# The opening of a hybrid decoder layer: token tiles ahead of weights, weight splits by halves, and one more load buffer

## The chip, the cores and the metric

One NeuronCore of a Trainium2 chip runs the whole program. The metric is the device time of one execution in microseconds (us), smaller is better. The kernel computes in float32 and takes each matrix product apart: every operand is split into an upper part (float32 rounded to the matrix engine's fp32r form) and a lower part (what is left), and a product is three passes: upper by upper, upper by lower, lower by upper.

Engines: PE is the matrix engine (its results go to PSUM banks), ACT the scalar engine, DVE the vector engine, POOL the general one, SP the queue that issues most loads.

## The reference

One layer on 512 tokens of 1024 channels:

```python
h = rms_norm(x, norm_mix_g)
p = h @ w_in                    # q_a, k_a, v_a, o_a, i_a, f_a, q_b, k_b, v_b, g_a, g_b
qk_a = silu(causal_conv(concat(q_a, k_a), conv_w))
h_a = mlstm_chunkwise(q_a, k_a, v_a, i_a + b_i, f_a + b_f)
y_a = sigmoid(o_a) * head_rms_norm(h_a)
y_b = stick_breaking(norm(q_b), norm(k_b), v_b)
y = sigmoid(g_a + b) * y_a + sigmoid(g_b + b) * y_b
x = x + y @ w_out
x = x + square(relu(rms_norm(x) @ w_up)) @ w_down
```

This case touches the first lines: the normalisation of x, its transposes, and the first column block of `v_a`, called va0; and the loads of the first q, k pairs of the second mixer, called qkb0.

## The kernel before, in words

Tokens lie in four tiles of 128 (t = 0 to 3). A tile's opening steps are: square and root on ACT with the reciprocal on DVE (`q`, L259 to L261); scaling by the root and by the gain on DVE in two halves of 512 channels (`s`, L267), each followed by four PE transposes into a bank `pt` (L271); the upper part of the turned half on ACT (`u`, L282) and the lower part on DVE (`l`, L286), both written into `hT`. Weights of va0 come in four pairs (256 rows of `w_in`, two k-slices of 128, 512 KB): the upper part is cast on ACT (`w`, L290), the lower part taken on DVE (`v`, L293). The gain is spread over the partitions by PE into two banks `gps` of the pool `ps_proj` (four banks), which the scaling reads until the last tile.

The order of these steps on ACT and DVE is written out as a string, which `opening` follows: each step is put behind the last one of its engine. Where PE's products stand is chosen by a planner from estimated times; `issue_after` and the argument `behind` add constraints. Engines then run their instructions in that order. `keep_warm(n)` issues n dummy products on a tile `warm` into the bank `pw`, of the pool `ps_a` (also four banks), after some of the transposes.

`chunk("va0", ...)` makes the products of va0 for one token tile o at a time as the planner sees it: eight k-slices of three passes (L120, L121, L122 of `mm3`), accumulated in a bank `pp`, then evacuated and split. Before the fourth tile come the products of the gates, `pg` (L316), which need the whole of `hT`.

SP issues the loads in program order of the planner: the gain `gx`, then for each i the token tile x i (L196) and the weight pair w i (`raw_va`, L198), then the columns of the gates (L367) and the pairs of the first mixer's q, k (`raw_qka`, L111).

Later, `stage` loads a pair into a buffer `raw`, and casts it (L115, L116). Up to qkb0 the buffers are two of the pool `wp`, in turn, so that the third pair is loaded after the first has been split. From qkb1 on a third buffer, in the pool `at`, takes part. The matrix products `za` of the first mixer (L452, L454), which read `qh`, `ql` and `kk`, start within the products of qkb1.

Of the kernel before, what the change touches and what calls it, by code (L numbers as in the profile page):

```python
# [8 lines left out]
F32 = mybir.dt.float32  # L9
F32R = mybir.dt.float32r  # L10
# [6 lines left out]
P = 128  # L17
S = 512
D = 1024
NT = S // P  # L20
NK = D // P
# [43 lines left out]
def block_kernel(ctx: ExitStack, tc: tile.TileContext, x, norm_mix_g, w_in, b_if, b_gate, conv_w, mlstm_norm_g,  # L65
                 sb_q_norm_g, sb_k_norm_g, w_out, norm_mlp_g, w_up, w_down, out):
    nc = tc.nc
    act, dve, pool, pe = nc.scalar, nc.vector, nc.gpsimd, nc.tensor
# [3 lines left out]
    wp = ctx.enter_context(tc.tile_pool(name="wp", bufs=4))  # L72
    r4 = ctx.enter_context(tc.tile_pool(name="r4", bufs=12))
    sm = ctx.enter_context(tc.tile_pool(name="sm", bufs=2))
    ps_proj = ctx.enter_context(tc.tile_pool(name="ps_proj", bufs=4, space=PSUM))
# [6 lines left out]
    def bank(name):  # L82
        return ps_a.tile([P, S], F32, tag="pa", name=name)
# [14 lines left out]
        return at.tile([P, S], F32, tag=tag, name=name, bufs=bufs)  # L98


    last, load_pool, staged = {}, [(wp, "raw", 2)], []

    def stage(k2, srcs, name, ahead=None, pool_raw=None):

        with tc.high_priority(offset=AHEAD if ahead is None else ahead):
            p, tag, bufs = load_pool[len(staged) % len(load_pool)] if pool_raw is None else (pool_raw, "raw", 2)
            staged.append(name)
            raw = p.tile([P, 2, 512], F32, tag=tag, name=f"raw_{name}{k2}", bufs=bufs)
            for c, ap in srcs:
                n = ap.shape[-1]  # L110
                last["load"] = nc.sync.dma_start(out=raw[:, :, c:c + n],  # L111
                                                 in_=ap.rearrange("(kk p) n -> p kk n", p=P)).ins
            hi = wp.tile([P, 2, 512], F32R, tag="whi", name=f"whi_{name}{k2}")
            lo = wp.tile([P, 2, 512], F32R, tag="wlo", name=f"wlo_{name}{k2}")
            act.copy(hi, raw)  # L115
            dve.tensor_sub(lo, raw, hi.bitcast(F32))  # L116
        return hi, lo

    def mm3(o, ah, al, bh, bl, start, stop, **kw):
        pe.matmul(o, ah, bh, start=start, stop=False, **kw)  # L120
        pe.matmul(o, ah, bl, start=False, stop=False, **kw)  # L121
        return pe.matmul(o, al, bh, start=False, stop=stop, **kw).ins  # L122

    def chunk(name, src, transposed, lhs=None, staged=None, evac=None, gen=False,
              order=range(4), behind={}):


        acc = {}

        def one(o, k, wh, wl):  # L130
            kk, sl = k % 2, slice(o * P, (o + 1) * P)
            st, sp = k == 0, k == NK - 1
            if transposed:
                mm3(acc[o], wh[:, kk, sl], wl[:, kk, sl], hT[0][:, k, :], hT[1][:, k, :], st, sp)
            else:
                ah, al = (hT[0][:, k, sl], hT[1][:, k, sl]) if lhs is None else lhs(k, sl)
                mm3(acc[o], ah, al, wh[:, kk, :], wl[:, kk, :], st, sp)

        def new(o):
            acc[o] = ps_proj.tile([P, S], F32, tag="pp", name=f"pp_{name}{o}")  # L140

        if evac is not None:
            w = staged or [stage(k2, src(k2), name) for k2 in range(4)]
            def each():
                for o in order:
                    new(o)
                    for k in range(NK):
                        with ExitStack() as es:
                            if k in behind:
                                es.enter_context(tc.issue_after(behind[k]))  # L150
                            one(o, k, *w[k // 2])
                    evac(o, acc[o])
                    yield
            if gen:
                return each()
            list(each())
        else:
            for o in range(4):
                new(o)
            for k2 in range(4):  # L160
                w = staged[k2] if staged else stage(k2, src(k2), name)
                for k in (2 * k2, 2 * k2 + 1):
                    for o in range(4):
                        one(o, k, *w)
        return list(acc.values())

    def in_cols(*parts):
        def src(k2):
            c, got = 0, []
            for c0, n in parts:  # L170
                got.append((c, w_in[0, k2 * 256:(k2 + 1) * 256, c0:c0 + n]))
                c += n
            return got
        return src
# [4 lines left out]
    def split(dst, val):  # L179

        act.copy(dst[:, 0, :], val)
        return dve.tensor_sub(dst[:, 1, :], val, dst[:, 0, :].bitcast(F32)).ins
# [3 lines left out]
    xp = first.enter_context(tc.tile_pool(name="xp", bufs=1, side="right"))  # L186
# [4 lines left out]
    gx = xp.tile([1, D], F32, name="gx")  # L191
    nc.sync.dma_start(out=gx, in_=norm_mix_g[0:1, :])
    xs, raw_va, va0_src = {}, {}, in_cols((C_VA, 512))
    for i in range(NT):
        xs[i] = xp.tile([P, D], F32, name=f"x_{i}")
        nc.sync.dma_start(out=xs[i], in_=x[0, i * P:(i + 1) * P, :])  # L196
        raw_va[i] = (xp if i < 2 else wp).tile([P, 2, 512], F32, tag="raw", name=f"raw_va0{i}", bufs=2)
        last["load"] = nc.sync.dma_start(out=raw_va[i], in_=va0_src(i)[0][1].rearrange("(kk p) n -> p kk n", p=P)).ins  # L198
    eps = cst.tile([P, 1], F32, name="eps")
    pool.memset(eps, EPS)  # L200
    one1 = xp.tile([P, P], F32R, name="one1")
# [25 lines left out]
    pw = bank("pw")  # L227

    def keep_warm(n):
        for i in range(n):  # L230
            pe.matmul(pw, warm[:, :P], warm, start=True, stop=True)
# [3 lines left out]
    for i in range(2):  # L235
        c = slice(i * S, (i + 1) * S)
# [9 lines left out]
    r_, xn_, pt_, va0_w, tail = {}, {}, {}, {}, {i.engine: i for i in (gain_hi, gain_lo)}  # L246

    def in_turn(f, *args):

        with ExitStack() as es:  # L250
            for i in tail.values():
                es.enter_context(tc.issue_after(i))
            for i in f(*args):
                tail[i.engine] = i
# [8 lines left out]
    def o_scale(t, g):  # L263
        if g == 0:
            xn_[t] = xp.tile([P, D], F32, tag="nx", name=f"xn{t}", bufs=3)
        c = slice(g * S, (g + 1) * S)
        yield dve.scalar_tensor_tensor(xn_[t][:, c], xs[t][:, c], r_[t], gps[g], ALU.mult, ALU.mult).ins  # L267
        pt_[t, g] = bank(f"pt{t}{g}")
        for i in range(4):
            k = 4 * g + i  # L270
            turned = pe.transpose(pt_[t, g][:, i * P:(i + 1) * P], xn_[t][:, k * P:(k + 1) * P], ident).ins  # L271
        last["turned", t, g] = turned
        with tc.issue_after(turned):
            keep_warm({(0, 0): 1, (0, 1): 5, (1, 0): 3}.get((t, g), 0))

    def h_part(t, g):
        return [h[:, 4 * g:4 * g + 4, t * P:(t + 1) * P] for h in hT], pt_[t, g][:, :].rearrange(
# [7 lines left out]
        (hi, lo), p3 = h_part(t, g)  # L285
        yield dve.tensor_sub(lo, p3, hi.bitcast(F32)).ins  # L286

    def o_weights(i):
        va0_w[i] = tuple(wp.tile([P, 2, 512], F32R, tag=f"w{w}", name=f"w{w}_va0{i}") for w in ("hi", "lo"))
        yield act.copy(va0_w[i][0], raw_va[i]).ins  # L290

    def o_weights_lower(i):
        yield dve.tensor_sub(va0_w[i][1], raw_va[i], va0_w[i][0].bitcast(F32)).ins  # L293

    def o_gates():
        for i in range(2):
# [4 lines left out]
    def opening(steps):  # L301
        kinds = {"q": o_square, "s": o_scale, "u": o_upper, "l": o_lower, "w": o_weights, "v": o_weights_lower,
                 "g": o_gates}
        with tc.high_priority(offset=URGENT):
            for n in steps.split():
                in_turn(kinds[n[0]], *(int(i) for i in n[1:]))
# [49 lines left out]
    v0, v1 = [], []  # L356

    def v_evac(got, name):
        def evac(o, acc):
            v = r4.tile([P, 2, S], F32R, tag="r4", name=f"{name}{o}")  # L360
            split(v, acc)
            got.append(v)
        return evac

    wr = cv.tile([P, NK, 16], F32, name="wg_r")
    with tc.issue_after(last["load"]):
        nc.sync.dma_start(out=wr, in_=w_in[0, :, C_I:C_I + 16].rearrange("(k p) n -> p k n", p=P))  # L367
    wg = r4.tile([P, 2, S], F32R, tag="r4", name="wg")[:, :, :].rearrange("p w (k n) -> p (w k) n", k=4)
    pool.memset(wg.bitcast(F32), 0.0)
    opening("q0 s00 s01 u00 l00 w0 v0 q1 s10 u01 l01 s11 u10 l10 w1 v1 u11 l11 q2 s20 s21 w2 v2 u20 l20 q3 s30 u21 "  # L370
            "s31 l21 w3 v3 u30 g l30 u31 l31")
    va0 = chunk("va0", None, False, staged=va0_w, evac=v_evac(v0, "va0"), gen=True,
                behind={k: last["turned", k // 2, 1] for k in range(4, NK)})
    next(va0)
    next(va0)
    next(va0)
# [267 lines left out]
    at = late.enter_context(tc.tile_pool(name="at", bufs=1, reuse_waits="tile"))  # L644
# [4 lines left out]
        pool.memset(oh[:, h, h:h + 1], 1.0)  # L649
    oh_r = at.tile([P, 8, 8], F32R, name="oh_r")  # L650
    pool.tensor_copy(oh_r, oh)
    msk = at.tile([P, S], F32, name="msk")
    pool.memset(msk, 0.0)
    pool.memset(msk[:, 384:], 1.0)
# [69 lines left out]
    def parts(n, t, own=False):  # L724
        hi, lo = (r4.tile([P, 2, S], F32R, tag="r4", name=f"w{w}_{n}") if own else
                  wp.tile([P, 2, S], F32R, tag=f"w{w}", name=f"w{w}_{n}") for w in ("hi", "lo"))
        act.copy(hi, t)
        dve.tensor_sub(lo, t, hi.bitcast(F32))  # L728
        return hi, lo
# [141 lines left out]
    with tc.high_priority(offset=AHEAD):  # L871
        w0 = [parts(f"p1up0{j}", buf0["X", j], True) for j in range(2)]
# [118 lines left out]
```

## Time and profile before

| | us |
|---|---|
| median of 3 runs (lowest, highest) | 816.85 (816.73, 817.37) |
| the profiled execution | 816.42 |
| its span, first to last instruction | 814.4 |
| PE busy | 805.7 |
| DVE busy | 599.8 |
| ACT busy | 457.1 |
| POOL busy | 164.6 |

A row of the timeline gives the start (us from the start of the span), the time of the group, engine, line, operation, the tile written and the tiles read, and how many instructions were merged; in brackets stand the idle time of the engine ahead of it and what ended it. A row of the windows gives the stretch, its length, busy time and count for PE, weight loads, DVE, ACT and POOL (an engine without work in the question asked is left out), the granted clock, the DMA share and GB/s. A row of the loads gives the target, the queue, the count, the size and the time from issue to landing. PE's matmuls are pipelined, and their ends are modelled: what one costs is the step from start to start.

### The profile page before, as it was taken

To read this page: it belongs to the slowest core of one execution; us is meant where nothing else is said; L and a number is where in the kernel's file an instruction comes from. 1 tells how busy PE (TensorE), PEld (TensorE's weight loads), DVE (VectorE), ACT (ScalarE), POOL (GpSimd) and SP (SyncE) were. 2 spreads that over 40 slices of the span, in tenths; PEclk is the share of its full clock that TensorE was granted. 3 is DMA by queue.
4 is the path that set the end of the run, shared out by engine and by line. 5 is a ranking of instruction groups with operands and counts; after the bars stand their busy time and mean duration, and the time that the engine had idled before them with its cause. 6 is when DMAs were issued, how large, how long until landed. Compare 5 with 4: busy or idle time off the path is not lost.

```text
span 814.4 us, 11569 instructions
## 1 busy us (share of the span) xinstructions
PE 805.7 (99%) x4392; PEld 693.5 (85%) x4392; DVE 599.8 (74%) x828; ACT 457.1 (56%) x681; POOL 164.6 (20%) x216
## 2 busy tenths in 40 slices
PE   8999999999999999999999999999999999999998
PEld 6878887888888887888888888999999899999876
DVE  6669967684598486756753659898689868978995
ACT  6429756654557467545542537576455635755642
POOL 3014323111221240010120101223302330232220
PEclk9999999999999999999999999999999999999999
DMA  9454542343433423522257506987977995999964
GB/s 225 98 155 147 123 77 63 88 98 85 150 93 93 120 62 70 137 72 77 78 182 263 124 1 158 208 177 159 204 228 161 179 208 182 182 198 184 233 120 119
DMA packets 64552, 113.65 MB, mean 140 GB/s; under 512 B 5809, under 2 KB 18401, under 8 KB 64498
## 3 DMA queue, kind: packets, MB, share of 16 engines
q1 hardware_dynamic: 44914, 71.43, 31.6%
q0 software_dynamic: 19584, 41.50, 26.8%
q8 instruction: 34, 0.56, 0.3%
q14 instruction: 20, 0.16, 0.1%
HBM read 110.74 MB, written 2.17 MB: 139 GB/s over the span
## 4 chain that ended last, share of the span: by engine, by line
PE 92%; DVE 5%; ACT 1%; issue 1%; DMA 0%; SPq 0%; DVEq 0%; ACTq 0%
PE pp_qkb L122 4%; PE pp_qkb L120 4%; PE pp_qkb L121 4%; PE pp_yup L120 3%; PE pp_yup L121 3%; PE pp_yup L122 3%; PE ydn L121 2%; PE ydn L122 2%; PE ydn L120 2%; PE pp_qka L120 2%; PE pp_va L121 2%; PE pp_qka L121 2%; PE pp_ga L121 2%; PE pp_vb L122 2%; PE pp_vb L120 2%; PE pp_oa L122 2%
## 5 line engine op out<-in xcount | busy, mean ns | idle before, releaser
L561 POOL TENSOR_SCALAR_AFFINE_SELECT b<-b 128x128 f32<-128x128 f32 x32 | 19.0, 608 | 161.2 <-ACT b L558 161.2
L121 PE MATMUL pp_qkb<-wlo_qkb,hT 128*128 128x512 f32 x128 | 50.2, 392 | 0.0
L122 PE MATMUL pp_qkb<-whi_qkb,hT 128*128 128x512 f32 x128 | 50.1, 394 | 0.0
L120 PE MATMUL pp_qkb<-whi_qkb,hT 128*128 128x512 f32 x128 | 49.4, 392 | 0.0
L767 POOL DMA_DIRECT2D raw_Xup<-in_w_up_dram x24 | 28.9, 1239 | 84.8 <-DVE wlo_p5up L728 37.2
L767 POOL DMA_DIRECT2D raw_Xdn<-in_w_down_dram x18 | 21.6, 1214 | 102.8 <-DVE wlo_p5dn L728 36.4
L566 DVE TENSOR_TENSOR_SCAN r<-r,msk 128x512 f32<-128x512 f32 (+3 forms) x32 | 25.1, 833 | 14.5 <-ACT r L558 14.5
L116 DVE TENSOR_TENSOR wlo_qkb<-raw_qkb,whi_qkb 128x1024 fp32r<-128x1024 f32 x16 | 21.7, 1364 | 13.8 <-ACT whi_qkb L115 13.8
L122 PEld LDWEIGHTS pp_qkb<-whi_qkb,hT 128*128 128x128 f32 x128 | 24.1, 188 | 5.1
L120 PEld LDWEIGHTS pp_qkb<-whi_qkb,hT 128*128 128x128 f32 x128 | 24.1, 188 | 5.1
L121 PEld LDWEIGHTS pp_qkb<-wlo_qkb,hT 128*128 128x128 f32 x128 | 24.1, 188 | 4.7
L913 ACT ACTIVATE uq<-uq 128x512 f32<-128x512 f32 x32 | 20.0, 630 | 12.2 <-DVE uq L912 12.0
L121 PE MATMUL pp_va<-wlo_va,hT 128*128 128x512 f32 x64 | 24.9, 392 | 0.8 <-DVE wlo_va L293 0.8
L120 PE MATMUL pp_ga<-hT,whi_ga 128*128 128x512 f32 x64 | 25.3, 395 | 0.0
L120 PE MATMUL pp_qka<-hT,whi_qka 128*128 128x512 f32 x64 | 25.2, 397 | 0.0
L121 PE MATMUL pp_qka<-hT,whi_qka 128*128 128x512 f32 x64 | 25.2, 394 | 0.0
L121 PE MATMUL pp_wo<-wlo_wo,y 128*128 128x512 f32 x64 | 25.1, 392 | 0.0
L121 PE MATMUL pp_ga<-hT,whi_ga 128*128 128x512 f32 x64 | 25.1, 392 | 0.0
L121 PE MATMUL pp_oa<-hT,whi_oa 128*128 128x512 f32 x64 | 25.1, 392 | 0.0
L122 PE MATMUL pp_oa<-hT,wlo_oa 128*128 128x512 f32 x64 | 25.1, 392 | 0.0
L120 PE MATMUL pp_vb<-whi_vb,hT 128*128 128x512 f32 x64 | 25.1, 392 | 0.0
L121 PE MATMUL pp_gb<-hT,whi_gb 128*128 128x512 f32 x64 | 25.1, 392 | 0.0
(578 smaller groups left out, 2962.1 us busy)
## 6 DMA issues: line engine op xcount, KB each, us to landing
raw_Xup<-in_w_up_dram POOLq DMA_DIRECT2D x24, 512.0 KB, 7.3
raw_Xdn<-in_w_down_dram POOLq DMA_DIRECT2D x18, 512.0 KB, 6.6
raw_qkb<-in_w_in_dram SPq DMA_DIRECT2D x32, 256.0 KB, 3.9
rb<-rows POOLq DMA_DIRECT2D x8, 640.0 KB, 5.5
raw_va<-in_w_in_dram SPq DMA_DIRECT2D x8, 512.0 KB, 5.2
raw_qka<-in_w_in_dram SPq DMA_DIRECT2D x16, 256.0 KB, 6.3
raw_vb<-in_w_in_dram SPq DMA_DIRECT2D x8, 512.0 KB, 4.4
raw_oa<-in_w_in_dram SPq DMA_DIRECT2D x8, 512.0 KB, 4.2
```

Source lines behind the costliest of these rows:

```text
L116: dve.tensor_sub(lo, raw, hi.bitcast(F32))
L120: pe.matmul(o, ah, bh, start=start, stop=False, **kw)
L121: pe.matmul(o, ah, bl, start=False, stop=False, **kw)
L122: return pe.matmul(o, al, bh, start=False, stop=stop, **kw).ins
L561: pool.affine_select(out=b[:, d], in_=b[:, d], pattern=[[-1, P]], compare_op=ALU.is_gt, fill=0.0, base=0, channel_multiplier=1)
L566: dve.tensor_tensor_scan(kr, kr, msk[:, S - n:][:, ::-1], 1.0, ALU.mult, ALU.max)
L767: pool.dma_start(out=buf[b, j], in_=src(more, j), accum_op=ALU.add)
L913: act.activation(h(r, c), h(r, c), AF.Square)
```

## The change

- The loads are issued as x0, x1, w0, w1, x2, w2, x3, w3 (before x0, w0, x1, w1, ...).
- In the string of steps, tile 1's square comes right after tile 0's on ACT, tile 1's scaling is mixed with tile 0's lower parts, and the pairs 0, 1 and 2 of the weights are cast and split by halves (one k-slice each: `w00`, `w01`, `v00`, `v01`).
- Within `mm3`, va0 makes the pass lower rows by upper weights ahead of upper rows by lower weights.
- The third tile's sums go to the bank `pw`, the dummies' one, instead of a new bank of `ps_proj`.
- The products of tile 1, k-slice 3, are put behind tile 2's first transposes on PE.
- After tile 0's second transposes stand three dummies instead of five.
- The third pair of qkb0 is loaded into the buffer of `at`.

```diff
+    last, load_pool, staged, at_once = {}, [(wp, "raw", 2)], [], {}
...
+            p, tag, bufs = at_once.get((name, k2), (p, tag, bufs))
...
-    def mm3(o, ah, al, bh, bl, start, stop, **kw):
+    def mm3(o, ah, al, bh, bl, start, stop, rows_first=False, **kw):
         pe.matmul(o, ah, bh, start=start, stop=False, **kw)
-        pe.matmul(o, ah, bl, start=False, stop=False, **kw)
-        return pe.matmul(o, al, bh, start=False, stop=stop, **kw).ins
+        two = ((ah, bl), (al, bh))
+        for i, (a, b) in enumerate(two[::-1] if rows_first else two):
+            end = pe.matmul(o, a, b, start=False, stop=stop and i == 1, **kw).ins
+        return end
...
-            acc[o] = ps_proj.tile([P, S], F32, tag="pp", name=f"pp_{name}{o}")
+            acc[o] = banks.get(o) or ps_proj.tile([P, S], F32, tag="pp", name=f"pp_{name}{o}")
...
-                            if k in behind:
-                                es.enter_context(tc.issue_after(behind[k]))
+                            for i in (k, (o, k)):
+                                if i in behind:
+                                    es.enter_context(tc.issue_after(behind[i]))
...
-    for i in range(NT):
-        xs[i] = xp.tile([P, D], F32, name=f"x_{i}")
...
+    for n in "x0 x1 w0 w1 x2 w2 x3 w3".split():
...
-            keep_warm({(0, 0): 1, (0, 1): 5, (1, 0): 3}.get((t, g), 0))
+            keep_warm({(0, 0): 1, (0, 1): 3, (1, 0): 3}.get((t, g), 0))
...
+    def o_weights(i, h=None):
+        if not h:
+            va0_w[i] = tuple(wp.tile([P, 2, 512], F32R, tag=f"w{w}", name=f"w{w}_va0{i}") for w in ("hi", "lo"))
+        c = slice(None) if h is None else slice(h, h + 1)
+        yield act.copy(va0_w[i][0][:, c], raw_va[i][:, c]).ins
...
-    opening("q0 s00 s01 u00 l00 w0 v0 q1 s10 u01 l01 s11 u10 l10 w1 v1 u11 l11 q2 s20 s21 w2 v2 u20 l20 q3 s30 u21 "
-            "s31 l21 w3 v3 u30 g l30 u31 l31")
-    va0 = chunk("va0", None, False, staged=va0_w, evac=v_evac(v0, "va0"), gen=True,
-                behind={k: last["turned", k // 2, 1] for k in range(4, NK)})
+    opening("q0 s00 s01 q1 u00 s10 l00 s11 w00 u10 v00 w01 l10 v01 u01 u11 l01 l11 w10 v10 w11 v11 q2 s20 s21 w20 u20 v20 "
+            "w21 l20 v21 q3 s30 s31 u21 l21 w3 v3 u30 g l30 u31 l31")
+    va0 = chunk("va0", None, False, staged=va0_w, evac=v_evac(v0, "va0"), gen=True, banks={2: pw}, behind={
+        **{k: last["turned", k // 2, 1] for k in range(4, NK)}, (1, 3): last["turned", 2, 0]})
...
+    at_once["qkb0", 2] = (at, "raw", 1)
```

More of the change, by code (lines that the diff above doesn't have):

```diff
@@ L98, in t2 @@
         return at.tile([P, S], F32, tag=tag, name=name, bufs=bufs)
-    last, load_pool, staged = {}, [(wp, "raw", 2)], []
+    last, load_pool, staged, at_once = {}, [(wp, "raw", 2)], [], {}
     def stage(k2, srcs, name, ahead=None, pool_raw=None):
@@ L117, in stage @@
         return hi, lo
-    def mm3(o, ah, al, bh, bl, start, stop, **kw):
+    def mm3(o, ah, al, bh, bl, start, stop, rows_first=False, **kw):
         pe.matmul(o, ah, bh, start=start, stop=False, **kw)
-        pe.matmul(o, ah, bl, start=False, stop=False, **kw)
-        return pe.matmul(o, al, bh, start=False, stop=stop, **kw).ins
+        two = ((ah, bl), (al, bh))
+        for i, (a, b) in enumerate(two[::-1] if rows_first else two):
+            end = pe.matmul(o, a, b, start=False, stop=stop and i == 1, **kw).ins
+        return end
     def chunk(name, src, transposed, lhs=None, staged=None, evac=None, gen=False,
-              order=range(4), behind={}):
+              order=range(4), behind={}, banks={}):
         acc = {}
@@ L136, in one @@
                 ah, al = (hT[0][:, k, sl], hT[1][:, k, sl]) if lhs is None else lhs(k, sl)
[L137 removed]
+                mm3(acc[o], ah, al, wh[:, kk, :], wl[:, kk, :], st, sp, name == "va0")
         def new(o):
[L140 removed]
+            acc[o] = banks.get(o) or ps_proj.tile([P, S], F32, tag="pp", name=f"pp_{name}{o}")
         if evac is not None:
@@ L193, in block_kernel @@
     xs, raw_va, va0_src = {}, {}, in_cols((C_VA, 512))
-    for i in range(NT):
-        xs[i] = xp.tile([P, D], F32, name=f"x_{i}")
-        nc.sync.dma_start(out=xs[i], in_=x[0, i * P:(i + 1) * P, :])
-        raw_va[i] = (xp if i < 2 else wp).tile([P, 2, 512], F32, tag="raw", name=f"raw_va0{i}", bufs=2)
-        last["load"] = nc.sync.dma_start(out=raw_va[i], in_=va0_src(i)[0][1].rearrange("(kk p) n -> p kk n", p=P)).ins
+    for n in "x0 x1 w0 w1 x2 w2 x3 w3".split():
+        i = int(n[1])
+        if n[0] == "x":
+            xs[i] = xp.tile([P, D], F32, name=f"x_{i}")
+            nc.sync.dma_start(out=xs[i], in_=x[0, i * P:(i + 1) * P, :])
+        else:
+            raw_va[i] = (xp if i < 2 else wp).tile([P, 2, 512], F32, tag="raw", name=f"raw_va0{i}", bufs=2)
+            last["load"] = nc.sync.dma_start(out=raw_va[i],
+                                             in_=va0_src(i)[0][1].rearrange("(kk p) n -> p kk n", p=P)).ins
     eps = cst.tile([P, 1], F32, name="eps")
@@ L286, in o_lower, with o_weights_lower @@
         yield dve.tensor_sub(lo, p3, hi.bitcast(F32)).ins
[L288 to L293, printed above, removed]
+    def o_weights(i, h=None):
[3 more added lines that the diff above has]
+        yield act.copy(va0_w[i][0][:, c], raw_va[i][:, c]).ins
+    def o_weights_lower(i, h=None):
+        c = slice(None) if h is None else slice(h, h + 1)
+        yield dve.tensor_sub(va0_w[i][1][:, c], raw_va[i][:, c], va0_w[i][0][:, c].bitcast(F32)).ins
     def o_gates():
```

## The prediction

> **What bounds the kernel now.** I read the page first, then the windows of the opening, then TensorE's timeline there, then ACT, DVE and the loads that feed it.
>
> ```profile
> span 814.4 us, 11569 instructions
> ...
> PE 805.7 (99%) x4392; PEld 693.5 (85%) x4392; DVE 599.8 (74%) x828; ACT 457.1 (56%) x681; POOL 164.6 (20%) x216
> ...
> PE 92%; DVE 5%; ACT 1%; issue 1%; DMA 0%; SPq 0%; DVEq 0%; ACTq 0%
> ```
>
> TensorE (PE) is busy for 99% of the span and makes 92% of the chain that ended last. A change elsewhere counts only if it takes idle time or needless products off PE. The windows show where PE is short of work:
>
> ```profile
> 0.00:5.00 5.00, 3.46 (x9) 2.81 (x10) 2.68 (x4) 2.81 (x4) 4.35 (x15) 1.00 0.59 155
> 5.00:10.00 5.00, 4.12 (x21) 2.79 (x20) 2.76 (x5) 3.04 (x6) 2.75 (x6) 1.00 1.01 224
> 10.00:15.00 5.00, 4.23 (x22) 3.18 (x22) 4.28 (x7) 3.72 (x8) 0.00 (x0) 1.00 1.01 242
> 15.00:20.00 5.00, 5.00 (x27) 4.13 (x26) 4.53 (x7) 3.51 (x6) 0.00 (x0) 1.00 1.05 273
> ```
>
> The second number is PE's busy time: from 15 us on PE is full. The DMA share (last but one) is 1.0 from 5 us on, so the opening's loads go as fast as they can, whatever their order. What can be won lies between the first token tile and about 15 us:
>
> ```profile
> 1.54 3.44 PE L231 MATMUL pw<-warm 128*128 128x512 f32 x8 [1.54 <-DVE warm L190]
> ...
> 7.25 0.66 PE L271 MATMUL pt<-ident,xn 128*128 128x128 f32 x4 [0.88 <-DVE xn L267]
> ...
> 8.33 1.41 PE L231 MATMUL pw<-warm 128*128 128x512 f32 x5
> ...
> 9.58 0.44 PE L120 MATMUL pp_va<-whi_va,hT 128*128 128x512 f32 x1
> ...
> 10.79 0.50 PE L121 MATMUL pp_va<-wlo_va,hT 128*128 128x512 f32 x1 [0.77 <-DVE wlo_va L293]
> ...
> 12.46 0.94 PE L231 MATMUL pw<-warm 128*128 128x512 f32 x3
> ...
> 31.25 3.79 PE L316 MATMUL pg<-hT,wg 128*128 128x512 f32 x16
> ```
>
> The first real product starts at 9.58, the second waits until 10.79 for the weights' lower part, and three dummies stand in the way at 12.46. The gate products (pg) start at 31.25; I use that start as the finish line of the opening. Between 9.58 and 31.25 stand these counts (first row the pp_va products, second the transposes) and, from the chain, what a group of four transposes takes:
>
> ```profile
> 9.50:31.20 21.70, 18.21 (x74) 13.46 (x74) 0.96 (x2) 1.17 (x2) 1.00 0.88 211
> 9.50:31.20 21.70, 3.57 (x24) 2.69 (x24) 4.81 (x7) 4.07 (x7) 1.00 0.88 211
> 12.22 0.49 PE pt L271 x4
> 25.51 0.44 PE pt L271 x4
> ```
>
> One product costs 0.227 us: the 16 pg take 3.79, less 0.39 for the last one's own length, over 15 steps. So 74 products are 16.8, six groups of transposes at 0.48 are 2.9, three dummies 0.7: 20.4 of the 21.67 us. Waiting is the rest, 1.27 us, nearly 1.0 of it the gap after 9.58. Waits and dummies together, 2.0 us, are all that can go behind the first product.
>
> **The change part by part. Loads.** These are issue times and the times to landing, in the order x0, w0, x1, w1, x2:
>
> ```profile
> 1.23 0.36 SPq L196 DMA_DIRECT2D x<-in_x_dram  x1
> x<-in_x_dram SPq DMA_DIRECT2D x1, 512.0 KB, 3.3
> 1.64 0.42 SPq L198 DMA_DIRECT2D raw_va<-in_w_in_dram  x1
> raw_va<-in_w_in_dram SPq DMA_DIRECT2D x1, 512.0 KB, 6.6
> 2.10 0.47 SPq L196 DMA_DIRECT2D x<-in_x_dram  x1
> x<-in_x_dram SPq DMA_DIRECT2D x1, 512.0 KB, 7.4
> 2.61 0.43 SPq L198 DMA_DIRECT2D raw_va<-in_w_in_dram  x1
> raw_va<-in_w_in_dram SPq DMA_DIRECT2D x1, 512.0 KB, 10.2
> 3.09 1.59 SPq L196 DMA_DIRECT2D x<-in_x_dram  x1
> x<-in_x_dram SPq DMA_DIRECT2D x1, 512.0 KB, 10.9
> ```
>
> Landings: x0 4.6, w0 8.2, x1 9.5, w1 12.8, x2 14.0. A token tile comes 1.2 to 1.3 us after what is ahead of it, a weight pair 3.3 to 3.6. With x1 ahead of w0, x1 lands near 5.9 (bounds 5.4 and 6.7) and w0 takes x1's old place, 9.5 (9.0 to 9.9). From w1 on the bytes ahead are the same. SP issues the same nine loads; only one swaps place, and the gate columns and first q, k loads behind them keep theirs.
>
> **Steps on ACT and DVE.** The chain of a tile, by tile 2, and the casts:
>
> ```profile
> 14.65 1.07 ACT L259 ACTIVATE jk<-x 128x1024 f32<-128x1024 f32 x1
> ...
> 16.37 1.41 DVE L267 SCALAR_TENSOR_TENSOR xn<-x,r,gps 128x512 f32<-128x512 f32 x2
> ...
> 8.42 1.05 ACT L290 CAST whi_va<-raw_va 128x1024 fp32r<-128x1024 f32 x1
> 9.51 1.23 DVE L293 TENSOR_TENSOR wlo_va<-raw_va,whi_va 128x1024 fp32r<-128x1024 f32 x1 [0.26 <-ACT whi_va L290]
> 88.37 0.62 ACT L461 CAST ph<-rb 128x512 fp32r<-128x512 f32 x1
> ...
> 127.56 0.68 DVE L462 TENSOR_TENSOR pl<-rb,ph 128x512 fp32r<-128x512 f32 x1
> ```
>
> From the start of a square to the start of the scaling is 1.72 us; one scaled half takes 0.75. Tile 0 runs as before (scaling 6.44 to 7.85). Tile 1's square follows tile 0's at once on ACT, near 6.15, so DVE can scale its first half at 7.9 and the transposes can start near 8.7. PE is through with the first six groups' dummies at 8.33 + 3 x 0.23 = 9.0; then come tile 1's first transposes (0.48), its three dummies (0.7) and, after the lower part l00 and the second scaled half on DVE (to 10.05), the second transposes: 10.2 to 10.75. The first half of w0 is cast by 9.5 + 0.6 = 10.1. So the first product starts near 10.8, 1.2 us later than now (bounds 10.1 and 11.4, from the bounds on x1 and w0), but tile 1's eight transposes and three dummies are behind it instead of ahead.
>
> Each half costs more than half: on ACT 2 x 0.62 against 1.05, on DVE, by the pl row, 2 x 0.68 against 1.23, that is 0.2 and 0.13 us more per pair, for three pairs. The Trainium skill speaks against halves here (Advanced Engine Details and Errata, The Read-Write Bubble: the memory latency shows between instructions, so large tiles are to be used). By that rule alone the opening would lose about 0.6 us on ACT and 0.4 on DVE; the trace agrees with the sign. I take nothing of it on PE's path, because ACT and DVE wait for loads in this stretch: w1's halves are cast 12.8 to 13.95, just ahead of x2 at 14.0. If that cover is gone (w1 0.5 us late) tile 2 is 0.5 us late.
>
> From 10.8 PE has k-slices 0 and 1 of two tiles, 12 products to 13.5, then slices 2 and 3 from w1 (first half at 13.4, second 13.95, lower parts 14.2 and 14.9). Of those, tile 1's slice 3, three products, is now held behind tile 2's first transposes. That leaves 9, to 15.6. Tile 2's transposes need x2 at 14.0 + 1.72 + 0.75 + 0.1 = 16.55. PE waits 0.95 us there (bounds 0.2, if x2 or its square comes earlier, and 1.7). Afterwards the held three run to 17.7, and w2's first half, cast by 17.0, brings the next twelve: no further wait.
>
> The third tile's own bank lets it start when its upper part is there (about 17.7) instead of when a gain bank is released by tile 3's scaling; tiles 0 and 1 still have work then, so I cost it at nothing, as I do the swap of the second and third product of a slice: the lower weights are there at 10.85. The two dummies taken out are inside the 9.0 above. The bank that no longer rotates leaves three for the transposes; tile 1's second group takes the first one, free after l00 at about 9.3: nothing.
>
> **Sum.** 10.8 + 16.8 (74 products) + 4 x 0.48 (remaining groups) + 0.95 = 30.5 against 31.25: 0.75 us saved. Behind it PE is full, so it should stay saved. The profiled execution took 816.42 us around its span of 814.4; that gives 815.7. The runs' median, 816.85, stands 0.4 higher, so I say 816.1.
>
> **The q, k buffer.** The third pair of qkb0 no longer waits for the first pair's split.
>
> ```profile
> 63.18 0.39 PE L120 MATMUL pp_qkb<-whi_qkb,hT 128*128 128x512 f32 x1
> ...
> 66.21 1.30 DVE L116 TENSOR_TENSOR wlo_qkb<-raw_qkb,whi_qkb 128x1024 fp32r<-128x1024 f32 x1
> ...
> 82.92 1.40 DVE L419 TENSOR_TENSOR ql<-cy,qh 64x512 fp32r<-64x512 f32 x2
> ...
> 85.17 0.39 PE L454 MATMUL za<-ql,kk 128*128 128x512 f32 x1
> ```
>
> The products start at 63.18 and use a pair for 24 x 0.227 = 5.45 us, so the fourth pair is needed near 79.5; its split ends at 67.5, 12 us ahead. The loads move, PE doesn't: nothing, bounds -0.3 and +0.8, the latter if a split gets ahead of the ql step, below.
>
> **The rivals.**
> *PE never waits for tile 2* (0.20). If the 0.95 us wait is filled (loads a little earlier, other products ahead of the transposes), the gain is 1.7 us: 815.15. For it: the three held products were ready. Against: the edit itself holds them.
> *Nothing gained* (0.16). x1 or w0 late, or the wait for tile 2 at its upper bound 1.7: 816.85. For it: the DMA share is 1.0, so the loads can't all win.
> *The clock drops* (0.05). The first eight dummies step by 0.43 us ((3.44 - 0.4)/7), twice 0.227, so PE does have a slow state, though the granted clock reads 1.00 there. A drop in the wait at 15.6, held for the 3 us seen at the start, makes 7 products of 13: 1.4 us lost, 817.5. Against: the idle stretches at 6.2 and 9.8, each about 1 us, left the step at 0.23. The Trainium skill (TensorE: Matmul & The Clock Gate, Part 1) has the half rate return after an idle window of about 3.4 us; the trace agrees so far.
> *Slower* (0.12). The orders on ACT and DVE are laid out anew; with the third pair early, more weight splits can be put on DVE ahead of ql. It ends at 84.3 now and PE uses it at 85.17, so the margin is 0.85. Each split ahead costs 1.23 us: two lose 1.6, which eats the gain and more; from three on (2.8 lost, 818.9) it is slower by over 0.2%. For it: DVE is packed there. Against: tiles for split weights come free only as PE goes on.
>
> **How the numbers follow.** The forecast case has 0.47, 816.1, its own range 815.3 to 816.9. Within 0.2% (1.63 us, about what a measurement can tell here) end the forecast, nothing gained and the clock: 0.68. Faster 0.20, slower 0.12. The range 814.8 to 817.6 takes in all but the slower case and some of the tails.
>
> **What would show it.** In the changed kernel's timeline: x1 landing near 5.9 and w0 near 9.5; the first pp_va product near 10.8 with tile 1's transposes ahead of it; one PE wait near 15.6 to 16.6, released by tile 2's xn; pg starting near 30.5; the step at 0.227 after that wait; za at its place less 0.75. It is wrong if pg starts after 31.2 or before 29.7, if PE's step doubles, or if a wait stands at za that isn't there now.

## The result, and the profile after

The changed kernel took 822.90 us (median of 4 runs, 822.66 to 823.32) where the kernel before took 816.79 (4 runs, 816.45 to 817.37) in the same comparison: a ratio of 1.0075, 95% interval 1.0057 to 1.0092. It is 6.1 us slower; forecast were 816.1 us and a range up to 817.6. The profiled execution took 823.32 us around a span of 821.3, 6.9 more than before.

From the page of the changed kernel, the span, the engines and the shares of the chain that ended last:

```profile
span 821.3 us, 11574 instructions
...
PE 808.0 (98%) x4390; PEld 694.8 (85%) x4390; DVE 598.6 (73%) x831; ACT 457.1 (56%) x684; POOL 160.2 (20%) x216
...
PE 90%; DVE 5%; DMA 3%; ACT 1%; issue 1%; SPq 0%; ACTq 0%; DVEq 0%
```

PE is busy for 2.3 us more than before, so some 4.6 of the 6.9 us are time without work. DMA, at 0% of the chain before, has 3% of it. Four of the windows of the changed kernel say where:

```profile
10.00:15.00 5.00, 5.00 (x26) 4.07 (x25) 4.41 (x8) 4.03 (x7) 0.00 (x0) 1.00 1.04 261
15.00:20.00 5.00, 4.01 (x22) 3.12 (x21) 3.49 (x7) 3.76 (x10) 0.00 (x0) 1.00 1.05 274
...
61.00:66.90 5.90, 1.76 (x8) 1.13 (x6) 0.48 (x1) 1.55 (x3) 4.23 (x16) 0.99 0.61 229
66.90:70.30 3.40, 3.37 (x8) 2.70 (x9) 3.37 (x7) 3.40 (x7) 1.50 (x3) 0.52 0.27 45
```

In the opening PE is now full from 10 us on, but for about 1 us behind 15. From 61 to 66.9 PE works 1.76 of 5.90 us, DVE 0.48 and ACT 1.55. From the end of PE's last product of qka0 (62.8) to the cast at 65.34 all three are still at once. In the 3.4 us behind that the granted clock is 0.52, and eight products fill them. The rows of PE's timeline, changed kernel:

```profile
10.40 0.40 PE L121 MATMUL pp_va<-whi_va,hT 128*128 128x512 f32 x1
...
15.19 0.61 PE L124 MATMUL pp_va<-wlo_va,hT 128*128 128x512 f32 x2
16.79 0.63 PE L279 MATMUL pt<-ident,xn 128*128 128x128 f32 x4 [0.99 <-DVE xn L275]
...
30.22 3.11 PE L327 MATMUL pg<-hT,wg 128*128 128x512 f32 x13
...
39.29 0.39 PE L121 MATMUL pp_qka<-hT,whi_qka 128*128 128x512 f32 x1
...
62.37 0.39 PE L124 MATMUL pp_qka<-hT,wlo_qka 128*128 128x512 f32 x1
66.93 0.79 PE L121 MATMUL pp_qkb<-whi_qkb,hT 128*128 128x512 f32 x1 [4.17 <-ACT xc L405]
...
70.37 0.40 PE L124 MATMUL pp_qkb<-whi_qkb,hT 128*128 128x512 f32 x1
```

The row of `pg` shows 13 of its 16 products, because this view ends at 33 us. The first product of qka0 in the kernel before:

```profile
39.86 0.39 PE L120 MATMUL pp_qka<-hT,whi_qka 128*128 128x512 f32 x1
```

qka0 is the first work that stands behind the whole opening, so its start compares equal work: 0.57 us earlier. That is one profile of each kernel; with the opening unchanged, qka0's start differs by 0.4 to 0.6 us between kernels (the table of marks below), so the size of this gain isn't firm. The loss comes at the border of qka0 and qkb0. From 62.37 to 66.93 are 4.56 us where a step is 0.227, a hole of 4.33; the eight products from 66.93 to 70.37 take 3.44 where full rate takes 1.82, that is 1.62 more. Less the 0.57 gained ahead of it, that makes 5.38 of the 5.65 us by which the first product of the last projection (wo) is late (454.93 against 449.28). Behind wo another 1.29 us come in. 1.10 of them arise between wo and the first product of `ydn` (589.23 against 582.48): PE waits 0.4 us there for ACT at `s1u`, near 560, which no other profile shows. The rest stays open; from wo's first product to PE's last the other kernels of this study differ by 0.84 us among themselves without any edit there.

What ended the hole, from the waits of the changed kernel between 44 and 70 us (us in total, times, longest), and ACT's timeline in it:

```profile
ACT whi_qkb L116 <- DMA raw_qkb<-in_w_in_dram: 14.1, 1, 14.1
PE pp_qkb L121 <- ACT xc L405: 4.2, 1, 4.2
```

```profile
50.14 1.05 ACT L116 CAST whi_qkb<-raw_qkb 128x1024 fp32r<-128x1024 f32 x1 [0.98 <-PE pp_qka L124]
65.34 1.04 ACT L116 CAST whi_qkb<-raw_qkb 128x1024 fp32r<-128x1024 f32 x1 [14.15 <-DMA raw_qkb<-in_w_in_dram]
66.30 1.56 ACT L405 COPY xc<-pp_qka 128x512 f32<-128x512 f32 x3
...
69.15 5.56 ACT L455 ACTIVATE rb<-rb,cc 128x512 f32<-128x512 f32 x12
```

The same stretch of ACT's timeline before:

```profile
57.72 1.05 ACT L115 CAST whi_qkb<-raw_qkb 128x1024 fp32r<-128x1024 f32 x1 [5.94 <-PE pp_qka L121]
61.34 1.95 ACT L393 COPY xc<-pp_qka 128x512 f32<-128x512 f32 x3 [2.58 <-PE pp_qka L122]
...
64.61 5.55 ACT L443 ACTIVATE rb<-rb,cc 128x512 f32<-128x512 f32 x12
```

The copies `xc` empty the banks of qka0's sums; qkb0's first product needs one of them. Before, they start at 61.34, as soon as PE has the sums. After, the cast of qkb0's third pair stands ahead of them and waits for its load until 65.34; the copies follow at 66.30 although their sums were long there. The Trainium skill (PSUM — Partial Sum Buffer, Engine vs sequencer instructions) calls the queues of ScalarE, VectorE and GpSimd strict first in, first out; the trace agrees, with a stop of 14.15 us ahead of the cast, in whose last 4 us ready copies stood behind it. The loads of the pairs (two DMAs of a pair in a row, median us from issue to landing), first the fourth and the third pair after, then the third before, and what SP waited for ahead of the third after:

```profile
51.00 1.00 SPq L112 DMA_DIRECT2D raw_qkb<-in_w_in_dram  x2
raw_qkb<-in_w_in_dram SPq DMA_DIRECT2D x2, 256.0 KB, 4.0
53.23 0.88 SPq L112 DMA_DIRECT2D raw_qkb<-in_w_in_dram  x2
raw_qkb<-in_w_in_dram SPq DMA_DIRECT2D x2, 256.0 KB, 11.6
```

```profile
52.01 1.00 SPq L111 DMA_DIRECT2D raw_qkb<-in_w_in_dram  x2
raw_qkb<-in_w_in_dram SPq DMA_DIRECT2D x2, 256.0 KB, 4.0
```

```profile
SPq L112 <- PE pc L356: 0.9, 1, 0.9
```

With its own buffer the third pair is not earlier but later. The memory of `at` lies under tiles of the steps before, so SP holds the load for the transposes `pc`, and then it goes out at 53.23, among three broadcasts of the decay rows (`rb`, 640 KB each) that POOL issues from 52.84 to 53.96. Before, the third pair went out at 52.01, into the buffer that the first had left and ahead of the decay rows (there from 53.74), and took 4.0 us.

### The profile page after: what moved, and what is told of

It is laid out like the page before. It is cut to its first block, busy times and chain, and to the rows that moved or that the text cites. A ratio compares the mean times of both kernels' runs of the same rounds, so it can differ in the third digit from the quotient of the medians.

```text
span 821.3 us, 11574 instructions
## 1 busy us (share of the span) xinstructions
PE 808.0 (98%) x4390; PEld 694.8 (85%) x4390; DVE 598.6 (73%) x831; ACT 457.1 (56%) x684; POOL 160.2 (20%) x216
## 4 chain that ended last, share of the span: by engine, by line
PE 90%; DVE 5%; DMA 3%; ACT 1%; issue 1%; SPq 0%; ACTq 0%; DVEq 0%
PE pp_qkb L124 7%; PE pp_yup L124 5%; PE ydn L124 4%; PE pp_qkb L121 4%; PE pp_ga L124 4%; PE pp_oa L124 4%; PE pp_vb L124 4%; PE pp_gb L124 4%; PE pp_xup L124 4%; PE pp_zup L124 3%; PE zdn L124 3%; PE pp_wo L124 3%; PE pp_qka L124 3%; PE pp_yup L121 3%; PE pp_va L124 3%; PE xdn L124 2%
## 5 line engine op out<-in xcount | busy, mean ns | idle before, releaser
L116 ACT CAST whi_qkb<-raw_qkb 128x1024 fp32r<-128x1024 f32 x16 | 16.8, 1053 | 20.7 <-DMA raw_qkb<-in_w_in_dram 14.1
```

## The experiments

Theory A: the third pair's cast, held by its late load, stops ACT ahead of the copies; the opening is innocent. Its rival: the opening's new orders cost the time themselves. From the third experiment on came theory G: the chain on ACT behind the copies (decay exponentials of four heads, then the sigmoids of the convolution) has no slack against PE, so whatever holds it takes back what the opening gains. The table at the end has each run's marks. Each kernel stands against the kernel before in its own comparison: 816.85 us (25 runs) for the first four, 817.33 (33) for the next four, 817.51 (27) for the next three, 817.72 (13) for the last. These medians of one kernel lie up to 0.9 us apart, so times from different groups compare only roughly.

**The opening alone** (after, without the buffer)

```diff
-    at_once["qkb0", 2] = (at, "raw", 1)
```

> The changed kernel without its last line: qkb0's third pair goes back to the two wp buffers; the whole opening stays. Theory A (the load buffer): the 4.3 us wait of PE before qkb0 in the changed kernel comes from the third pair's load, which waits for memory under its new buffer, is queued with the three decay-row loads, lands at 65, and whose cast stands ahead of the copies that free qka0's banks. Without it the third pair is early again; but SP's order now has the fourth pair behind a first half-load into the at buffer, which waits for the same memory, and the fourth cast stands ahead of the last of the four copies. So A expects pg at 30.2 as in the changed kernel, a smaller wait (2 to 3 us) for the last bank, in all 818 to 820. Theory B (the opening itself costs, by the order it gives to everything behind it): 822 to 823 again, with the 4.3 us wait. Theory C (neither; the opening's gain is simply kept): 815.8.

819.22 us (9 runs), ratio 1.0027 [1.0018, 1.0037]. The time is the one that theory A expected, but not by the wait of 2 to 3 us that it expected: no wait stands ahead of qkb0 now. The opening is not free either. ACT's timeline:

```profile
65.38 1.05 ACT L116 CAST whi_qkb<-raw_qkb 128x1024 fp32r<-128x1024 f32 x1 [2.82 <-DMA raw_qkb<-in_w_in_dram]
66.33 0.58 ACT L405 COPY xc<-pp_qka 128x512 f32<-128x512 f32 x1
66.81 5.55 ACT L455 ACTIVATE rb<-rb,cc 128x512 f32<-128x512 f32 x12
```

The planner, with its times shifted by the opening, puts a first half of qkb1 (bound for `at`, so held by `pc` too) ahead of the fourth pair on SP. The fourth pair's cast is late in its turn and holds the last copy and the exponentials: 66.81 against 64.61 before. The products of qkb0 start 0.73 earlier than before, yet wo starts 2.04 later.

**The buffer alone** (before, with the buffer)

```diff
+            p, tag, bufs = at_once.get((name, k2), (p, tag, bufs))
...
+    at_once["qkb0", 2] = (at, "raw", 1)
```

> The kernel before with the last line of the change alone: qkb0's third pair into the at buffer, the old opening. Theory A: the load of the third pair is issued near 54 when the transposes of pc are done, lands near 65 beside the decay rows, and PE waits some 4 us for qka0's banks and then runs some products at half its rate: 816.8 + 4 to 6 = 821 to 823. Theory B: 816.5 to 817.2, no wait.

822.32 us (4 runs), ratio 1.0062 [1.0048, 1.0076]: nearly the whole loss. Its waits between 55 and 140 us hold one line for PE:

```profile
PE pp_qkb L121 <- ACT xc L394: 4.0, 1, 4.0
```

Theory A holds: the opening has no part in this wait, and eight products at half rate follow it here too.

**The third cast behind the copies** (after, one order on ACT added)

```diff
-            act.copy(hi, raw)
+            with ExitStack() as es:
+                if (name, k2) in after_cast:
+                    es.enter_context(tc.issue_after(after_cast[name, k2]))
+                act.copy(hi, raw)
...
+                after_cast["qkb0", 2] = got["qka0"][4]
```

> The changed kernel, with the cast of qkb0's third pair put behind the last copy of qka0's sums on ACT; its load is as late as in the changed kernel. If the wait is ACT's order (the copies queued behind a cast that waits for a load, theory A), PE has its banks as soon as qka0 ends, near 62.5; the third pair, landing at 65, is cast by 66.5 and needed near 73: no wait, 815.5 to 816.5. If the late load itself is what costs (DMA contention delaying the weights that PE needs, theory D), PE still waits 4 us, 821 to 823.

818.88 us (9 runs), ratio 1.0025 [1.0015, 1.0035]. The wait is gone, qkb0 starts at 62.85, and still the time is 2 us above the expectation, which was a miss. ACT's timeline and, between 55 and 140 us, PE's only wait:

```profile
61.01 2.63 ACT L408 COPY xc<-pp_qka 128x512 f32<-128x512 f32 x4 [9.56 <-PE pp_qka L127]
65.04 2.00 ACT L119 CAST whi_qkb<-raw_qkb 128x1024 fp32r<-128x1024 f32 x2 [1.40 <-DMA raw_qkb<-in_w_in_dram]
66.95 5.55 ACT L458 ACTIVATE rb<-rb,cc 128x512 f32<-128x512 f32 x12
```

```profile
PE pt_qT L552 <- ACT yq L488: 1.6, 1, 1.6
```

The late casts now hold the exponentials instead of the copies, and PE waits 40 us later, at 102.6, for ACT. This gave theory G.

**The opening with the loads in the order of before**

```diff
-    at_once["qkb0", 2] = (at, "raw", 1)
...
+                    if name == "qkb1":
+                        es.enter_context(tc.issue_after(last["qkb0", 3]))
```

> The changed kernel without its last line, and with qkb1's loads put behind the last of qkb0's on SP, as they stood before. Theory A: all qkb0 loads are early, no wait before qkb0, so the opening's gain of 1.0 us (pg at 30.2 against 31.25) stays to the end: 815.5 to 816.2. Theory B: a wait stays before qkb0, 820 or more. If the later waits of the changed kernel near 560 (0.6 us) come from the shifted order, 816.5 to 816.9 instead.

816.50 us (11 runs), ratio 0.9997 [0.9988, 1.0005]. This is the opening without its side effect on SP. The time is 0.3 above theory A's range and 0.4 from the forecast, but it doesn't bear the forecast out: the interval contains one, and in its profile qka0 starts only 0.13 and wo 0.01 earlier than before. The exponentials start at 64.72 (before 64.61).

**The buffer elsewhere** (after, third buffer in a pool of its own, opened ahead of `at`)

```diff
+                    if (name, k2) == ("qkb0", 2):
+                        es.enter_context(tc.issue_after(last["qkb0", 1]))
...
+    a0 = late.enter_context(tc.tile_pool(name="a0", bufs=1, reuse_waits="tile"))
...
-    at_once["qkb0", 2] = (at, "raw", 1)
+    at_once["qkb0", 2] = (a0, "raw", 1)
...
-            load_pool[:] = [(wp, "raw", 2), (at, "raw", 1), (wp, "raw", 2)]
+            load_pool[:] = [(wp, "raw", 2), (a0, "raw", 1), (wp, "raw", 2)]
```

> The changed kernel, with the third pair's buffer at the lower end of the new memory (a pool opened ahead of at), where nothing earlier lies, and its load put behind the second pair's on SP. Theory A (the buffer's memory comes free late, and the load then falls among the decay rows): the third pair is issued right behind the second, near 42, lands before 50, no wait of PE before qkb0; the opening's small gain stays: 816.0 to 817.0. Rival E (a third buffer at qkb0 is harmful wherever it lies, because the order of the later loads and casts changes): a wait before qkb0 or near 100 stays, 818 or more.

817.13 us (10 runs), ratio 1.0001 [0.9992, 1.0011], 0.1 above the range expected. The third pair, whose load this version also puts right behind the second pair's, lands at 46.5, and the 5.8 us are back: it was the place of the buffer and the late load that came of it, not the number of buffers. Of a gain there is nothing, though qkb0 starts 0.43 earlier than before. ACT's exponentials (the first and the last row) and POOL's masks of the same rows:

```profile
64.18 2.54 ACT L459 ACTIVATE rb<-rb,cc 128x512 f32<-128x512 f32 x5
...
71.02 0.51 ACT L459 ACTIVATE rb<-rb,cc 128x256 f32<-128x256 f32 x1 [0.29 <-POOL rb L453]
```

```profile
65.13 5.86 POOL L453 TENSOR_SCALAR_AFFINE_SELECT rb<-rb 128x128 f32<-128x128 f32 x8
```

ACT starts them early and then waits for POOL; the sigmoids start at 72.84, 1.37 later than before. ACT's chain is late for another reason, and wo is late with it.

**Decay rows cut short** (after, a tenth of the bytes for three of the four heads)

```diff
+        n0 = 128 if h < 3 else LIN
+        nc.gpsimd.dma_start(out=rb[:, :n0], in_=rows[h:h + 1, :n0].partition_broadcast(P))
+        if h < 3:
+            pool.memset(rb[:, n0:], -1.0)
```

> The changed kernel; for heads 0 to 2 only 128 of the 1280 columns of each decay row are loaded (64 KB instead of 640 KB) and POOL fills the rest with a constant, so that part of the result is not the layer's. The third pair's load is issued as late as in the changed kernel, near 53, but without the 1.9 MB beside it. If the contention makes the lateness (the load takes 12 us instead of some 4), it lands near 57 to 58, is cast before qka0 ends, no wait before qkb0: 815.5 to 818. If the late issue alone decides (theory F), the wait stays at 4 us: 821 to 823.

816.96 us (10 runs), ratio 0.9996 [0.9986, 1.0005]. The load of the third pair between 53.5 and 54.3, its landing time, and the cast:

```profile
raw_qkb<-in_w_in_dram SPq DMA_DIRECT2D x2, 256.0 KB, 5.9
```

```profile
60.02 1.05 ACT L116 CAST whi_qkb<-raw_qkb 128x1024 fp32r<-128x1024 f32 x1 [8.46 <-DMA raw_qkb<-in_w_in_dram]
61.12 1.95 ACT L405 COPY xc<-pp_qka 128x512 f32<-128x512 f32 x3
```

Issued as late as in the changed kernel (53.59, there 53.23), it lands after 5.9 instead of 11.6 us, and the cast is done when the copies are due. So the late issue alone would have done no harm; the decay rows beside it make the 4 us.

**The hold on va0 taken out** (the version with loads in order, without the edit that puts three of tile 1's products behind tile 2's transposes)

```diff
-        **{k: last["turned", k // 2, 1] for k in range(4, NK)}, (1, 3): last["turned", 2, 0]})
+        **{k: last["turned", k // 2, 1] for k in range(4, NK)}})
```

> The opening with qkb0's loads in order (as in the run that did that), without the hold of tile 1's slice 3 behind tile 2's first transposes. In the runs with the hold, the first qka0 product starts 25.18 us after x2 lands (13.97 and 39.14, 14.10 and 39.29, 14.37 and 39.54, 14.54 and 39.73): PE waits for tile 2. Without the hold the three products run inside that wait; theory: the start comes 0.3 to 0.7 us earlier, 24.5 to 24.9 us after x2, and the time is 815.8 to 816.4. Rival: the three products are missing behind the first transposes, where PE then waits for the second half of tile 2: 25.2 as before, 816.5.

816.99 us (11 runs), ratio 0.9994 [0.9985, 1.0003]. From the landing of x2 to qka0 it needs 24.65 us; the seven kernels that share the changed kernel's opening need 25.17 to 25.19. So the hold costs 0.53 us of the opening. The time, 0.6 above the range expected, doesn't show it: the fourth pair is issued 0.6 earlier than in the version with loads in order, but its second half lands after 11.7 us instead of 9.9 (why, no run tells). Its cast starts at 64.55 instead of 63.28, the exponentials at 65.98, and wo 1.2 after its place of before.

**Whole casts** (the version with loads in order; the three weight pairs cast and split whole)

```diff
-    opening("... s10 l00 s11 w00 u10 v00 w01 l10 v01 u01 u11 l01 l11 w10 v10 w11 v11 q2 ...")
+    opening("... s10 l00 s11 w0 u10 v0 l10 u01 u11 l01 l11 w1 v1 q2 ...")
```

> The opening with qkb0's loads in order, with w0, w1 and w2 cast and split whole instead of by halves. Theory: as long as ACT is through with w1 when x2 lands, halves cost nothing and whole casts delay the first slice by about 0.45 us on ACT and 0.5 us on DVE at w0, w1 and w2; but PE waits for tile 2 near 16 anyway, so 25.2 us from x2 to the first qka0 product, up to 25.6 if the lower part of w2 is late; 816.4 to 817.0. Rival (halves pay a fixed cost per instruction on the path, whole casts are better): 24.8 or less, below 816.2.

817.52 us (10 runs), ratio 1.0004 [0.9995, 1.0013]. qka0 starts 25.42 behind x2 instead of 25.18: the halves are worth 0.24 us to the opening. The time, 0.5 above the range expected, says nothing of them: the fourth pair's cast waits for its load until 64.89, and wo is 1.6 later than before.

**No hold, and the fourth cast behind two heads' exponentials**

```diff
+CAST_BEHIND = (("qkb0", 3),)
...
+                if (name, k2) in CAST_BEHIND:
+                    es.enter_context(tc.issue_after(last["exp", 1]))
```

> The opening, qkb0's loads in order, no hold, and the cast of qkb0's fourth pair behind the decay exponentials of heads 0 and 1 on ACT. In the runs so far the first sigmoid after qka0 and the first product of the output projection (wo) stand 377.6 to 377.8 us apart when PE waits near 95 to 104, and without such waits wo follows the first qkb0 product by 386.1 to 386.2. Theory G (ACT's chain from the copies of qka0's sums over the exponentials to the sigmoids is as long as PE's work beside it; whatever holds it up by more than PE's start came earlier is paid): with the fourth cast out of the chain the sigmoids start by 71.0, the early end of qka0 (62.2) stays a gain: 815.9 to 816.4, and no waits at 95 to 104. Rival (the decay rows' loads and POOL's selects hold the exponentials anyway): the sigmoids at 72 or later, 816.8 to 817.3.

815.80 us (11 runs), ratio 0.9982 [0.9973, 0.9991]: with that of the last kernel below, the only interval that lies wholly under one. The sigmoids start at 70.62, by 71.0 as theory G expected. ACT's timeline:

```profile
60.27 2.63 ACT L413 COPY xc<-pp_qka 128x512 f32<-128x512 f32 x4 [2.57 <-PE pp_qka L132]
62.80 3.74 ACT L463 ACTIVATE rb<-rb,cc 128x512 f32<-128x512 f32 x8
66.44 1.04 ACT L124 CAST whi_qkb<-raw_qkb 128x1024 fp32r<-128x1024 f32 x1
67.38 1.93 ACT L463 ACTIVATE rb<-rb,cc 128x512 f32<-128x512 f32 x4
```

No load stands in the chain any more: copies, then exponentials at 62.80, and the cast at a place where its load has landed. qkb0 and wo both start 1.05 to 1.06 earlier than before: here the opening's gain stays whole.

**The same cast moved in the kernel before**

```diff
+CAST_BEHIND = (("qkb0", 3),)
...
+                if (name, k2) in CAST_BEHIND:
+                    es.enter_context(tc.issue_after(last["exp", 1]))
```

> The kernel before, with the cast of qkb0's fourth pair behind the decay exponentials of heads 0 and 1. Theory G: before, the chain on ACT just keeps up with PE, so taking a cast of 1 us out of it gives nothing: 816.6 to 817.1, the first product of wo near 449.3. Rival (the chain already costs time in the kernel before): 815.9 or less.

817.16 us (10 runs), ratio 0.9996 [0.9987, 1.0006]. By itself the move brings nothing: qkb0 starts at 63.18 as before, and wo at 449.29. In the same comparison the version above is 1.36 us faster, so that gain is the opening's, with the cast out of its way. What a shorter chain on ACT would bring in the kernel before, this run doesn't tell: its exponentials start earlier (63.86 against 64.61), but with the cast between them the sigmoids don't (71.68 against 71.47).

**The changed kernel with both casts moved**

```diff
+CAST_BEHIND = (("qkb0", 2), ("qkb0", 3))
```

> The changed kernel, its late third pair included, with the casts of the third and fourth pairs of qkb0 behind the decay exponentials of heads 0 and 1 on ACT. In the run with the cast behind the last copy alone, the exponentials still stood behind two casts that waited for the loads (66.95 instead of 64.6), and 2.0 us were lost. Theory G: the loads land at 65 as ever, the casts follow near 68, PE needs them at 73 and 79; the exponentials start near 64, no wait before qkb0 and none near 95 to 104 beyond 0.5 us: 816.2 to 817.0. Rival (the late load costs elsewhere too, in DVE's queue or by contention): 818 or more.

817.36 us (11 runs), ratio 0.9999 [0.9991, 1.0008]. The buffer stays in `at`, and the load is as late as ever (65.1); ACT's order alone gives back 5.5 us (the time is 0.4 above the range expected):

```profile
60.89 2.62 ACT L409 COPY xc<-pp_qka 128x512 f32<-128x512 f32 x4 [9.56 <-PE pp_qka L128]
63.41 3.74 ACT L459 ACTIVATE rb<-rb,cc 128x512 f32<-128x512 f32 x8
67.05 1.99 ACT L120 CAST whi_qkb<-raw_qkb 128x1024 fp32r<-128x1024 f32 x2
```

With two casts between the exponentials the sigmoids start at 72.17, and wo is 0.54 later than before.

**The third tile's own bank taken out** (of the fastest version)

```diff
-    va0 = chunk("va0", ..., gen=True, banks={2: pw}, behind={
+    va0 = chunk("va0", ..., gen=True, behind={
```

> The version without the hold on va0 and with the cast of qkb0's fourth pair behind the decay exponentials (815.80 us), but with the third tile's sums in a bank of the projections again instead of the dummies' bank. It tells what that bank of its own is worth, which the prediction costed at nothing. If nothing, the time is that of the version it comes from, 815.4 to 816.4 us, and the first product of qka0 stands 24.7 us behind the landing of the third tile as there. If the third tile's sums have to wait for a bank that the second tile's transposes hold, TensorE lacks work between 15 and 22 us, the first product of qka0 comes up to 0.7 us later behind that landing, and the time is 816.3 to 816.9 us.

816.35 us (10 runs), ratio 0.9986 [0.9976, 0.9995]. From x2 to qka0 25.09 us instead of 24.70. PE's timeline shows two short stops ahead of transposes:

```profile
17.11 1.22 PE L287 MATMUL pt<-ident,xn 128*128 128x128 f32 x8 [0.35 <-DVE xn L283]
...
21.29 0.65 PE L287 MATMUL pt<-ident,xn 128*128 128x128 f32 x4 [0.20 <-DVE xn L283]
```

In the trace the bank is worth 0.39 us to this opening, which has no hold. The time doesn't decide: 816.35 lies in both ranges expected, and across two comparisons the intervals overlap.

Marks of the profiled execution of each kernel: starts (us) of the first product of qka0 and of qkb0, of the first sigmoid of the convolution and of the first product of wo, and two distances.

| kernel | qka0 | qkb0 | sigmoid | wo | wo less qkb0 | wo less sigmoid |
|---|---|---|---|---|---|---|
| before | 39.86 | 63.18 | 71.47 | 449.28 | 386.10 | 377.81 |
| after | 39.29 | 66.93 | 76.02 | 454.93 | 388.00 | 378.91 |
| opening alone | 39.14 | 62.45 | 73.67 | 451.32 | 388.87 | 377.65 |
| buffer alone | 40.28 | 67.67 | 79.76 | 455.58 | 387.91 | 375.82 |
| third cast behind | 39.54 | 62.85 | 73.81 | 451.16 | 388.31 | 377.36 |
| loads in order | 39.73 | 63.03 | 71.58 | 449.27 | 386.24 | 377.70 |
| buffer elsewhere | 39.45 | 62.75 | 72.84 | 450.52 | 387.77 | 377.68 |
| short decay rows | 39.65 | 62.96 | 71.25 | 449.07 | 386.11 | 377.82 |
| no hold | 39.15 | 62.45 | 72.84 | 450.47 | 388.01 | 377.62 |
| whole casts | 39.47 | 62.78 | 73.19 | 450.87 | 388.09 | 377.69 |
| no hold, cast moved | 38.81 | 62.12 | 70.62 | 448.23 | 386.12 | 377.62 |
| before, cast moved | 39.91 | 63.18 | 71.68 | 449.29 | 386.11 | 377.61 |
| after, casts moved | 39.42 | 62.73 | 72.17 | 449.82 | 387.09 | 377.65 |
| no bank of its own | 39.51 | 62.81 | 71.31 | 448.92 | 386.11 | 377.61 |

Theory G in these columns: wo comes no earlier than 386.1 us behind qkb0's first product (PE's own work) and, but for two kernels, no earlier than 377.6 behind the first sigmoid (ACT's chain and what hangs on it). Where one distance is above its floor, the other is at it. In the kernel before both are, within 0.2 us. In the two kernels with the half-rate stretch (after, buffer alone) PE's floor plus the 1.6 us of that stretch gives wo to 0.3 us; the buffer alone has its sigmoids in another order, so its last column doesn't compare. The third cast behind, with 377.36, lies 0.25 below the floor; why, no run tells.

PE's timelines show where the time behind qkb0 goes. Between 71 and 120 us, the steps that are over 0.15 us too long add up to 2.3 us in the opening alone, 2.1 in the third cast behind, 1.5 in the buffer elsewhere, 1.8 in no hold, 1.9 in whole casts and 0.9 in after, casts moved. All stand between 93 and 106 us. The waits named there are for DVE (`pl`, `nat`) in four of the six and for ACT (`yq`) in two, so what hangs on the sigmoids is not ACT's work alone. The six kernels with 386.1 or 386.2 in the fifth column have no such step.

## Why the prediction was wrong

- **The loads, right.** x1 landed at 6.06 and w0 at 9.32 (forecast 5.9 and 9.5).
- **The first product, right.** 10.40 against 10.8 (bounds 10.1 and 11.4), with tile 1's first transposes ahead of it at 9.26 and the second only 0.46 behind it.
- **The wait for tile 2, right.** One wait where it was put, from 15.65 (15.42, the second of the row at 15.19, and a step) to 16.79: 1.14 us against 0.95. The step behind it was 0.227.
- **The opening's sum, near.** pg starts at 30.22 (forecast 30.5), but with 72 of va0's products ahead of it, not 74. By qka0 the gain is 0.57 against 0.75.
- **Costs of nothing in the opening.** The bank of the third tile was put at nothing and is worth 0.39 (in the version without the hold). The halves, put at nothing on PE's path, gain 0.24 there; the 0.6 us on ACT and 0.4 on DVE that halves were to cost by the Trainium skill (Advanced Engine Details and Errata, The Read-Write Bubble) did not reach PE. That section counts 512 elements, the size of the halves, among the large tiles too, so it speaks against them less than the prediction takes it to. The hold, which the first rival doubted, costs 0.53.
- **"The loads move, PE doesn't: nothing", the step that failed.** It read only when PE needs the fourth pair (near 79.5, its split 12 us ahead, in the kernel before) and took it for granted that the third pair's load would come earlier. The load landed later, and PE waited not for its weights but for the banks behind its cast. Three things were left out: what the buffer's memory waits for, what else is loading then, and what stands behind the cast on ACT. The bound of +0.8 was taken from a split ahead of ql, and that of -0.3 has no reason beside it; the hole measured 4.33 us and the half-rate stretch 1.62. The buffer alone shows it without the opening; short rows, buffer elsewhere and both casts moved each take away one of the three, and each takes the time back to that of before.
- **"Behind it PE is full, so it should stay saved", the second failure.** A full PE tells that its work is the bound so far, not that other chains have slack. ACT's chain at 61 to 72 us had none: in the opening alone, the buffer elsewhere, no hold and whole casts PE was ahead at qkb0 by 0.4 to 0.7 us and behind at wo by 1.2 to 2.0. In the version with loads in order there was little to keep: qka0 is 0.13 ahead, because x2 landed 0.5 late there, and wo 0.01. Where nothing held the chain, the gain at qka0 was kept to wo: 1.05 us in no hold, cast moved, 0.36 in no bank of its own, 0.21 in short decay rows.
- **The rivals.** The slower case came with a mechanism that none of them had: no wait stands at za, and PE nowhere waits for ql. The clock rival's mechanism is real, but struck at 66.9, behind another wait; in the opening 1.14 us of idling left the clock alone. Its price of 1.4 us for a drop was near the 1.62 measured.

## What to carry to other kernels

Before a load is moved to another buffer, three rows are to be read: what frees that buffer's memory, what else is in flight at its new issue time, and which instructions stand behind the first user of the data on its in-order engine. A cast that waited for a load belonged, in this kernel, behind the copies that free PSUM banks, and out of the chain that had no slack. Where PE is 99% busy, a second chain can be just as long: measure the distance from each chain's marks to a common later mark in a few variants, and the one at its floor is the bound.

## What the runs showed of the hardware

- Behind the hole of 4.17 us without work, eight products took 0.43 us a step, with a granted clock of 0.52 in their window, for 3.44 us; behind gaps of 0.99 and 1.6 us (changed kernel at 16.79, third cast behind at 102.6) no half rate followed. The Trainium skill (TensorE: Matmul & The Clock Gate, Part 1) gives an idle window of about 3.4 us and a busy one of the same length; the trace agrees with both.
- A pair's two DMAs of 256 KB landed after 4.0 us where the first was issued 1.7 or 1.8 us ahead of the first decay row, and after 11.6 beside three of 640 KB; with a tenth of their bytes for three heads, after 5.9.
- A mask of 128x128 on POOL took 0.25 us while DVE idled (four in 1.02 us, three times, changed kernel from 60.89 on) and 0.73 beside DVE's convolution (eight in 5.86, the row above; eight in 5.60 before). That DVE's work slows it was not tested by itself.
- The opening before starts qka0 at 39.86, 39.91 and 40.28 in three profiles with the same opening code. What goes with it is the square of tile 1 on ACT, at 9.54, 9.62 and 9.97, behind the landing of x1 (9.5, 9.6 and 9.9). PE's half rate at the start also lasts longer in the last (beyond 6 us, in the first to 4.8), but its first transposes are only 0.12 later (7.37 against 7.25), while tile 1's first transposes are 0.43 later (12.48 against 12.05), as its square is. In the new opening the landing of x2 (13.97 to 14.54) sets the start of qka0 one to one, 25.18 us later.
